# Row sums of squares from token-major rows, and a planner that only asks for order between matmuls of one PSUM tile

## The chip, the cores and the metric

The kernel runs on one core of a Trainium2 chip. The metric is the device time of one execution in microseconds (us), the median of several runs. The core's engines are TensorE (PE, with PEld for its weight loads), VectorE (DVE), ScalarE (ACT), GpSimd (POOL) and SyncE (SP); each runs its own instructions in program order and waits for the others by semaphores. ACT, POOL and SP also issue DMA transfers.

## The reference

One decoder layer on x of 2048 tokens by 1024 features, all in float32, cut to what matters here:

```
n    = rms_norm(x, norm_w)                 # x * rsqrt(mean(x*x) + 1e-6) * norm_w, per token
proj = n @ w_in                            # pool u, z; q, k, v, z of 4 heads; b, a (4 + 4 columns)
y_pool = pool_mixer(u, z)                  # causal means over 2, 4, 8, 16 tokens, a 128x128 map, SiLU gate
y_dn   = gated delta rule(q, k, v, b, a)   # 4 heads of 128, short convolution, a state per head
h    = x + concat(y_pool, y_dn) @ w_out
out  = rms_norm(h, final_norm_w)
```

The factor rsqrt(mean(x*x) + 1e-6) is one number per token. The projection doesn't wait for it: it multiplies x times norm_w by the weights, and the factor is applied to the result.

## The kernel before, in words

The 2048 tokens are two batches b of 1024, and a batch is two halves hf of 512. x comes feature-major (the input xT, features on partitions): `load_x` brings a half of a batch in four transfers of 512 KB (the first one in two pieces), `split_x` makes for each of its eight blocks of 128 features a rounded part nh (ACT, L518) and a remainder nl (DVE, L519). `project` adds into one PSUM tile ps, for each of these eight k, three matmuls of 128x512: nh by wh (L725), nl by wh (L726) and nh by wl (L727), where wh and wl are the two parts of a 128-column tile of the weight (wh from a transfer on POOL's queue, wl from ACT L716 and a transfer that adds).

The row sums: `square_x` squares each of the eight blocks on ACT (L527, L531) and adds it to the sum sacc on DVE (odd k) or POOL (even k, L533). `row_scale` sums sacc over the partitions with four one-column matmuls into pss (L538), takes the mean (DVE L542) and rsqrt (POOL L500), and makes a diagonal matrix dg per 128 tokens (DVE L549, it needs the identity, which is the first part of the constants cst). `broadcast` turns dg by a matmul into psr (L553) and ACT copies it to rb (L555): the factor of every token on all partitions. Everything that leaves a projection's PSUM tile is multiplied by rb, so the first of these waits for it. `gate_rows` makes the b and a columns in psba (L561, L562) with the weights whl, which ACT and DVE make from wba (L488, L489); `gate_scale` multiplies them by rb (ba, L566) and `gate_turn` transposes them on PE (L573).

After the projections of a head come its chunks of the delta rule, whose state passes through PE, ACT and DVE in turn (PE ch and ob, ACT nv, o and the squares sqj, DVE v and state; L993 to L1022). At the end the output projection works on pairs of token tiles in products M1 to M7, whose sums lie in the PSUM tiles psA to psD; DVE adds x (L1295), ACT squares with a sum (L1297), POOL takes the rsqrt (L500), and the scaled rows go out on SP's queue.

The order of the instructions is made by a planner in Python. The kernel gives pieces of work to `at(slot, fn, ...)`; they are traced by slot. The class `Planner` then plays the program by a table of costs (`costs`): each engine takes, of what is ready, the instruction with the earliest due time; PE takes whole runs (the matmuls of one piece), looking at most REACH = 24 runs ahead. An instruction counts as ready when all it depends on has ended by the table (`preds`) or, for some pairs, has begun (`begun`). The order that comes out is what each engine runs. It sets no time: on the chip an engine waits for what it really needs. Transfers on SP and ACT share eight lanes, each with a semaphore: a new transfer on a lane is issued when the last one on it has landed.

Of the kernel before, what the change touches and what calls it, by code (L numbers as in the profile page):

```python
# [7 lines left out]
F32 = mybir.dt.float32  # L8
# [29 lines left out]
L_RB = (5.5, 4.25, 5.25, 4.25)  # L38
L_MIX, WARM = 90, 11
L_ROW, L_GROW, L_SUMS, L_DEC = 3.0, 2.5, 2, 4.0  # L40
L_KK, L_Q, L_QK, L_SPLIT, L_W = 1.5, 6.5, 1.5, 20, 30
L_ROW0, L_SQ1, L_SQB, L_X, L_GR0, L_GR, L_GCOL = (16.0, 18.0), 13.5, -40, 44, 21.5, 5.5, 2.75
PAIRED = 2

X_TAGS = (
    (("dec", 4), ("dec", 4), ("dec", 4), ("kdec", 2)),
    (("dec", 4), ("kdec", 2), ("kT", 2), ("kT", 2)),
)
WO_TAGS = (("At",), ("Ai",), ("Tt", 2), ("vT",))
# [37 lines left out]
class Planner:  # L87
# [34 lines left out]
    def costs(self, i, outs, ins):  # L122
# [27 lines left out]
        if eng == "Pool":  # L150
            t = 600 if op == "TensorTensor" and n <= NC else {"TensorScalarAffineSelect": 620}.get(op, 0.95 * n if op == "Memset" else 2.5 * n + 20)
            return t, t + 30
# [11 lines left out]
    def run(self):  # L164
# [56 lines left out]
        after = [[] for _ in range(N)]  # L221
        for k, p in enumerate(preds):
            begun[k] -= p | {k}
            for j in p:
                succs[j].append(k)
            for j in begun[k]:
                after[j].append(k)
# [169 lines left out]
def hymba_kernel(  # L397
# [31 lines left out]
    def st(shape, dt, tag, bufs=1):  # L429
        return plan.tile(sp, shape, dt, tag, tag, bufs)  # L430
# [36 lines left out]
    def load_constants():  # L467
        plan.opening = len(plan.traced)
        tri = st([P, 2, P], F32, "X")
        for dst, src in (  # L470
            (cst, consts[:, 0:C_TMP]),
            (wba, w_ba),
# [49 lines left out]

    def square_x(k, env):
        xk = env["x"][k // 2][:, k % 2]
        if k == 0:
            env["ss"] = ss = st([P, HALF], F32, "sacc", 2)
            nc.scalar.activation(ss, xk, AF.Square)  # L527
        else:
            ss = env["ss"]
            sq = st([P, HALF], F32, "acc", 3)  # L530
            nc.scalar.activation(sq, xk, AF.Square)  # L531
            eng = nc.vector if k % 2 else nc.gpsimd
            eng.tensor_tensor(out=ss, in0=ss, in1=sq, op=ALU.add)  # L533

    def row_scale(env):
        ps = plan.tile(pd, [P, HALF], F32, "pd", "pss", 2, True)
        for j in range(NCH):
            nc.tensor.matmul(  # L538
                ps[:, j : j + 1], env["ss"][:, j * P : (j + 1) * P], ones[:, 0:1], start=True, stop=True
            )  # L540
        v = st([P, NCH], F32, "ms", 2)
        nc.vector.tensor_scalar(  # L542
            out=v, in0=ps[:, 0:NCH], scalar1=1.0 / D, scalar2=EPS, op0=ALU.mult, op1=ALU.add
        )
        r = st([P, NCH], F32, "rstd", 2)
        rsqrt(r, v)
        env["dg"] = dg = st([P, NCH, P], F32, "sacc", 2)
        for j in range(NCH):
            nc.vector.tensor_scalar(out=dg[:, j], in0=ident, scalar1=r[:, j : j + 1], scalar2=None, op0=ALU.mult)  # L549

# [120 lines left out]
    def at(slot, fn, *args):  # L671
        events.append((slot, len(events), fn, args))
# [434 lines left out]
    tri = []  # L1107
    at(-90, begin)
    at(-89, warm_up)
    at(-45, lambda: tri.append(load_constants()))  # L1110
    at(-1, lambda: prepare_constants(tri[0]))
    for b in range(NB):
# [21 lines left out]
        for hf in range(NHALF):  # L1134
# [4 lines left out]
            for k in range(KT):  # L1139
                at(base + 0.1 + k * (8 * PAIRED - 2) / KT, split_x, k, env)  # L1140
                at(base + (L_SQB if b else 4 + L_SQ1 * hf) + k * (8 * PAIRED - 2) / KT, square_x, k, env)
            base += 8 * PAIRED - 2
            base += L_ROW if b else L_ROW0[hf]
            at(base, row_scale, env)
            at(base + L_RB[b * NHALF + hf], broadcast, env)
# [403 lines left out]
```

## Time and profile before

| | us |
|---|---|
| median of 3 runs (lowest, highest) | 940.88 (939.42, 942.4) |
| the profiled execution | 942.56 |
| span of its profile | 940.9 |
| PE busy | 917.2 (97%) |
| DVE, ACT, POOL busy | 617.1 (66%), 471.1 (50%), 188.2 (20%) |

The span is the time between the first and the last record of the profile; 1.66 us of the execution lie around it. Starts are counted from the span's start. A row of a timeline gives the start, the time that the instruction took, its engine, its line, what it writes and reads, and in brackets how long its engine had been idle before it and what ended that. Matmuls overlap: two of 128x512 that follow one another start 0.23 us apart though each shows 0.39.

### The profile page before, as it was taken

Reading aid. Unit: us, or ns where it says so; the run is one execution under the profiler, and the core shown is the slowest. Engines: PE = TensorE matmul, PEld = TensorE weight load, DVE = VectorE, ACT = ScalarE, POOL = GpSimd, SP = SyncE. Lnnn points to the kernel's source line nnn. Section 1 sums busy time; section 2 is a strip of 40 time slices with the busy share of each in tenths; the row PEclk is TensorE's granted clock in tenths of the full one; section 3 lists DMA queues with packets and bytes.
Section 4 is the critical chain, followed back from the end, with each engine's and each line's share of the span. In section 5 each row is a group of like instructions: output and inputs, shape, how many; then the busy total and the mean of one; then the engine's idle time right before and its main releaser. Section 6 shows DMA issues by size and latency. Waiting matters only on the chain.

```text
span 940.9 us, 14732 instructions
## 1 busy us (share of the span) xinstructions
PE 917.2 (97%) x5226; PEld 739.0 (79%) x5226; DVE 617.1 (66%) x1637; ACT 471.1 (50%) x1225; POOL 188.2 (20%) x224
## 2 busy tenths in 40 slices
PE   8999999999999999999999999999999999999995
PEld 5678888778878878768887787887887788788884
DVE  7476867666758545855785675855854477976553
ACT  8348555464454345624945546545533345444442
POOL 3417210110110113312720121111011101112221
PEclk9999999999999999999999999999999999999998
DMA  8425564344333454433445244353248487376554
GB/s 291 106 57 115 132 167 104 65 96 92 85 91 95 122 181 138 109 74 83 102 95 125 56 88 107 71 107 95 60 111 259 121 230 227 128 187 161 153 112 123
DMA packets 82265, 115.81 MB, mean 123 GB/s; under 512 B 31888, under 2 KB 49552, under 8 KB 82192
## 3 DMA queue, kind: packets, MB, share of 16 engines
q0 software_dynamic: 17280, 56.89, 28.3%
q1 hardware_dynamic: 64480, 57.46, 19.8%
q8 instruction: 41, 0.67, 0.3%
q10 hardware_dynamic: 432, 0.53, 0.2%
q14 instruction: 32, 0.26, 0.1%
HBM read 92.83 MB, written 22.02 MB: 122 GB/s over the span
## 4 chain that ended last, share of the span: by engine, by line
PE 67%; issue 11%; DVE 8%; DMA 6%; POOL 3%; ACT 3%; SPq 1%; DVEq 0%; POOLq 0%; ACTq 0%
PE ps L725 13%; PE ps L727 12%; PE ps L726 12%; DMA wh<-in_w_in_dram 2%; PE psA L1403 2%; PE psA L1404 2%; PE psA L1402 2%; PE ch L1009 1%; PE ch L1015 1%; PE tp L817 1%; PE ch L993 1%; PE ob L1003 1%; PE kk L843 1%; PE psC L1404 1%; PE psC L1402 1%
## 5 line engine op out<-in xcount | busy, mean ns | idle before, releaser
L725 PE MATMUL ps<-nh,wh 128*128 128x512 f32 x768 | 325.9, 424 | 1.4 <-ACT wh L713 0.8
L726 PE MATMUL ps<-nl,wh 128*128 128x512 f32 x768 | 301.6, 393 | 2.2 <-DVE nl L519 2.1
L727 PE MATMUL ps<-nh,wl 128*128 128x512 f32 x768 | 301.6, 393 | 0.0
L727 PEld LDWEIGHTS ps<-nh,wl 128*128 128x128 f32 x768 | 144.6, 188 | 32.1 <-DVE wl L503 0.4
L725 PEld LDWEIGHTS ps<-nh,wh 128*128 128x128 f32 x768 | 145.4, 189 | 27.4 <-issue 1.7
L726 PEld LDWEIGHTS ps<-nl,wh 128*128 128x128 f32 x768 | 145.5, 189 | 27.1 <-DVE nl L519 4.5
L739 DVE SCALAR_TENSOR_TENSOR acc<-u,cw,acc 128x512 f32<-128x512 f32 x144 | 109.6, 761 | 17.2 <-ACT acc L737 15.3
L708 POOL DMA_DIRECT2D wh<-in_w_in_dram x40 | 23.2, 579 | 289.9 <-PE ps L727 278.3
L734 DVE TENSOR_TENSOR u<-ps,rb 128x512 f32<-128x512 f32 x48 | 33.1, 689 | 59.7 <-PE ps L727 59.6
L717 POOL DMA_DIRECT2D wl<-in_w_in_dram x40 | 35.1, 878 | 155.8 <-ACT wl L716 100.6
L716 ACT ACTIVATE wl<-wh 128x1024 fp32r<-128x1024 f32 x40 | 42.4, 1059 | 34.7 <-DMA wh<-in_w_in_dram 31.3
L896 DVE TENSOR_TENSOR tmp<-Ai,X 128x60 f32<-128x60 f32 (+24 forms) x248 | 53.5, 216 | 7.7 <-DMA Ai<-blocks 1.5
L902 DVE TENSOR_TENSOR X<-X,tmp 128x60 f32<-128x60 f32 (+24 forms) x248 | 53.7, 216 | 6.7
L737 ACT ACTIVATE acc<-u,cw 128x512 f32<-128x512 f32 x48 | 34.8, 724 | 42.3 <-DVE u L734 41.7
L1022 ACT ACTIVATE sqj<-v 128x128 f32<-128x128 f32 x64 | 19.8, 309 | 64.5 <-DVE v L1020 59.7
L1016 DVE SCALAR_TENSOR_TENSOR state<-state,ex,ch 128x128 f32<-128x128 f32 x64 | 22.0, 344 | 28.1 <-PE ch L1015 27.7
L1410 POOL DMA_DIRECT2D dec<-in_x_dram x23 | 20.0, 871 | 100.6 <-ACT dec L1409 58.9
L1011 ACT ACTIVATE nv<-ch,sm 128x128 f32<-128x128 f32 x64 | 23.6, 368 | 30.4 <-PE ch L1009 30.0
L824 ACT ACTIVATE sqj<-tp 128x128 f32<-128x128 f32 x128 | 33.6, 280 | 4.2 <-PE tp L817 3.9
L1005 ACT ACTIVATE o<-ob,ex 128x128 f32<-128x128 f32 x64 | 23.5, 367 | 13.7 <-PE ob L1003 13.2
L993 PEld LDWEIGHTS ch<-state,kT 128*128 128x128 f32 x128 | 22.5, 188 | 8.3 <-DVE state L1016 4.3
L1015 PEld LDWEIGHTS ch<-nv,kdec 128*128 128x128 f32 x128 | 19.7, 188 | 11.7 <-ACT nv L1011 11.0
(288 smaller groups left out, 1760.3 us busy)
## 6 DMA issues: line engine op xcount, KB each, us to landing
wh<-in_w_in_dram POOLq DMA_DIRECT2D x40, 512.0 KB, 3.9
wl<-in_w_in_dram POOLq DMA_DIRECT2D x40, 512.0 KB, 5.6
y_dram<-yt SPq DMA_DIRECT2D x32, 256.0 KB, 3.1
out_dram<-dec SPq DMA_DIRECT2D x14, 512.0 KB, 4.5
dec<-in_x_dram POOLq DMA_DIRECT2D x23, 256.0 KB, 4.2
Ai<-blocks SPq DMA_DIRECT2D x32, 128.0 KB, 2.7
yr<-y_dram SPq DMA_DIRECT2D x8, 512.0 KB, 4.5
dec<-in_xT_dram SPq DMA_DIRECT2D x7, 512.0 KB, 6.9
```

The source lines that it names most:

```text
L716: nc.scalar.activation(w["lo"], w["hi"].bitcast(F32), AF.Copy, scale=-1.0)
L717: nc.gpsimd.dma_start(w["lo"], w_in[et], accum_op=ALU.add)
L725: nc.tensor.matmul(ps, w["hi"][:, k], nh[:, k], start=(k == 0), stop=False)
L726: nc.tensor.matmul(ps, w["hi"][:, k], nl[:, k], start=False, stop=False)
L727: nc.tensor.matmul(ps, w["lo"][:, k], nh[:, k], start=False, stop=(k == KT - 1))
L734: nc.vector.tensor_tensor(out=ub[:, HALO:], in0=ps, in1=rb, op=ALU.mult)
L737: nc.scalar.activation(acc, ub[:, HALO:], AF.Copy, scale=cw[:, ci, CONV - 1 : CONV])
L739: nc.vector.scalar_tensor_tensor(out=acc, in0=ub[:, h0 + j : h0 + j + HALF], scalar=cw[:, ci, j : j + 1], in1=acc, op0=ALU.mult, op1=ALU.add,)
L824: nc.scalar.activation(junk, tp[:, j], AF.Square, accum_out=dst[:, c : c + 1])
L896: nc.vector.tensor_tensor(out=tmp[:, 0:n, 0:w], in0=Ai[:, j, j + 1 : BS].unsqueeze(1).to_broadcast([P, n, w]), in1=X[:, 0:n, j : j + 1].to ...
L902: nc.vector.tensor_tensor(out=X[:, 0:n, j + 1 : BS], in0=X[:, 0:n, j + 1 : BS], in1=tmp[:, 0:n, 0:w], op=ALU.subtract)
L993: nc.tensor.matmul(ch[:, 0], res["kT"][:, t], S, start=True, stop=True)
```

## The change

Three things are changed.

- Row sums. `square_x` and the matmuls into pss are gone. `load_rows` loads x once more, token-major (128 tokens on partitions, 1024 features, 512 KB per transfer, four per half, on SP's queue), and `square_rows` squares such a tile on ACT with a sum along the row, which gives the four columns of ms. In the first batch the tiles take buffers that are not yet used (ROW_TAGS); in the second all eight go through the one buffer yr1, one after the other. `row_scale` now only makes the mean and the rsqrt, in the second batch 36 slots earlier than before; `row_diagonal` makes dg where `row_scale` made it.
- The identity (in cst) is loaded at the start on ACT's queue, not among the constants on SP's.
- The planner. A matmul that adds to or follows another on PE by data now counts as ready when the other has begun, by the table, and no longer when it has ended. And a small TensorTensor on POOL (the rsqrt) costs 430 + 160 n ns in the table for n columns, 600 before.

```diff
+ROW_TAGS = (
+    (("Ai",), ("At",), ("v0",), ("vT",)),
+    (("Tt", 2), ("Tt", 2), ("yr1",), ("Ai",)),
+)
...
-            t = 600 if op == "TensorTensor" and n <= NC else {"TensorScalarAffineSelect": 620}.get(op, 0.95 * n if op == "Memset" else 2.5 * n + 20)
+            t = 430 + 160 * n if op == "TensorTensor" and n <= NC else {"TensorScalarAffineSelect": 620}.get(op, 0.95 * n if op == "Memset" else 2.5 * n + 20)
...
         for k, p in enumerate(preds):
+            if eng[k] == "PE":
+                own = {j for j in p if eng[j] == "PE"}
+                p -= own
+                begun[k] |= own
             begun[k] -= p | {k}
...
         for dst, src in (
-            (cst, consts[:, 0:C_TMP]),
             (wba, w_ba),
...
-    def square_x(k, env):
...
+    def load_rows(b, hf, j, env):
+        env["xt", j] = xt = st([P, D], F32, *(ROW_TAGS[hf][j] if b == 0 else ("yr1",)))
+        t0 = b * TB + hf * HALF + j * P
+        nc.sync.dma_start(xt, x[t0 : t0 + P, :])
+
+    def square_rows(j, env):
+        if j == 0:
+            env["ms"] = st([P, NCH], F32, "ms", 2)
+        xt = env["xt", j]
+        nc.scalar.activation(xt, xt, AF.Square, accum_out=env["ms"][:, j : j + 1])
 
     def row_scale(env):
-        ps = plan.tile(pd, [P, HALF], F32, "pd", "pss", 2, True)
-        for j in range(NCH):
-            nc.tensor.matmul(
-                ps[:, j : j + 1], env["ss"][:, j * P : (j + 1) * P], ones[:, 0:1], start=True, stop=True
-            )
...
+        v = env["ms"]
+        nc.vector.tensor_scalar(out=v, in0=v, scalar1=1.0 / D, scalar2=EPS, op0=ALU.mult, op1=ALU.add)
+        env["r"] = r = st([P, NCH], F32, "rstd", 2)
         rsqrt(r, v)
+
+    def row_diagonal(env):
         env["dg"] = dg = st([P, NCH, P], F32, "sacc", 2)
...
+    at(-79.5, lambda: nc.scalar.dma_start(cst, consts[:, 0:C_TMP]))
...
-                at(base + (L_SQB if b else 4 + L_SQ1 * hf) + k * (8 * PAIRED - 2) / KT, square_x, k, env)
...
-            at(base, row_scale, env)
+            for j in range(NCH):
+                at(base - L_XT + 4 * j if b else -67 + 5 * hf + 0.1 * j, load_rows, b, hf, j, env)
+                at(base - L_XT + 8 + 4 * j if b else 4 + 8 * hf + j, square_rows, j, env)
+            at(base - L_XT + 24 if b else base, row_scale, env)
+            at(base, row_diagonal, env)
```

What the planner makes of this is seen from the order of the instructions. SP's queue in the opening, after the loads of xT and of the first weight (dec, kdec and kT hold xT), before:

```order
L513 DMA kT<-in_xT_dram 128x2x512 x2
L481 DMA cst<-in_consts_dram 128x192
L481 DMA wba<-in_w_ba_dram 128x64
L481 DMA pw<-in_pool_w_dram 128x512
L481 DMA psc<-in_pool_scale_dram 128x4
L481 DMA dtb<-in_dt_bias_dram 128x4
```

and after (Ai, At, v_146 and vT hold the rows of the first half, both Tt, yr_154 and the later Ai those of the second):

```order
L520 DMA kT<-in_xT_dram 128x2x512 x2
L533 DMA Ai<-in_x_dram 128x1024
L533 DMA At<-in_x_dram 128x1024
L533 DMA v_146<-in_x_dram 128x1024
L533 DMA vT<-in_x_dram 128x1024
L533 DMA Tt<-in_x_dram 128x1024 x2
L533 DMA yr_154<-in_x_dram 128x1024
L488 DMA wba<-in_w_ba_dram 128x64
L533 DMA Ai<-in_x_dram 128x1024
L488 DMA pw<-in_pool_w_dram 128x512
```

Seven loads of rows now stand ahead of wba. ACT in the opening, from the second half's split of x on, before:

```order
L518 ACTIVATE nh<-dec,nw 128x512
L518 ACTIVATE nh<-kdec,nw 128x512 x2
L518 ACTIVATE nh<-kT,nw 128x512 x2
L488 CAST whl<-wba 128x8x8
L518 ACTIVATE nh<-kT,nw 128x512 x2
L716 ACTIVATE wl<-wh 128x1024
L531 ACTIVATE acc<-dec 128x512
L527 ACTIVATE sacc<-dec 128x512
```

and after:

```order
L719 ACTIVATE wl<-wh 128x1024
L525 ACTIVATE nh<-kT,nw 128x512 x2
L539 ACTIVATE Ai,ms<-Ai 128x1024
L539 ACTIVATE At,ms<-At 128x1024
L495 CAST whl<-wba 128x8x8
L539 ACTIVATE v_146,ms<-v_146 128x1024
L539 ACTIVATE vT,ms<-vT 128x1024
L525 ACTIVATE nh<-kT,nw 128x512 x2
L539 ACTIVATE Tt,ms<-Tt 128x1024 x2
```

The cast of wba stands ahead of the last two squares of the first half and of the last two splits (k = 6, 7 of the second half). PE at the program's end, the last nine matmuls before:

```order
L1402 MATMUL psA<-At,wh 128x512
L1403 MATMUL psA<-Tt,wh 128x512
L1404 MATMUL psA<-At,wl 128x512
L1402 MATMUL psC<-nh,rb 128x512
L1403 MATMUL psC<-nl,rb 128x512
L1404 MATMUL psC<-nh,acc 128x512
L1402 MATMUL psA<-Ai,wh 128x512
L1403 MATMUL psA<-vT,wh 128x512
L1404 MATMUL psA<-Ai,wl 128x512
```

and after (psC's three rows then stand three times more, up to the end):

```order
L1409 MATMUL psA<-Ai,wh 128x512
L1410 MATMUL psA<-vT,wh 128x512
L1411 MATMUL psA<-Ai,wl 128x512
L1409 MATMUL psC<-nh,rb 128x512
L1410 MATMUL psC<-nl,rb 128x512
L1411 MATMUL psC<-nh,acc 128x512
```

Before, the two tiles took turns to the end; after, psA is finished twelve matmuls ahead of it. The same holds in the projections: among all neighbours in PE's order that belong to a projection or to the output products there were 809 changes of the PSUM tile, and are 196.

## Rows read from the trace of the kernel before

**Rows 1.** The page: busy time, share of the span and instructions of each engine.
```profile
PE 917.2 (97%) x5226; PEld 739.0 (79%) x5226; DVE 617.1 (66%) x1637; ACT 471.1 (50%) x1225; POOL 188.2 (20%) x224
```
**Rows 2.** Timeline, PE in the opening: start, duration, instruction, idle before and releaser.
```profile
5.97 0.50 PE L725 MATMUL ps<-nh,wh 128*128 128x512 f32 x1 [0.75 <-ACT wh L713]
...
14.60 0.50 PE L726 MATMUL ps<-nl,wh 128*128 128x512 f32 x1 [0.72 <-DVE nl L519]
...
18.94 0.50 PE L726 MATMUL ps<-nl,wh 128*128 128x512 f32 x1 [0.64 <-DVE nl L519]
...
21.67 0.40 PE L727 MATMUL ps<-nh,wl 128*128 128x512 f32 x1
...
21.90 0.95 PE L538 MATMUL pss<-ones,sacc 128*128 128x1 f32 x8
...
23.02 0.39 PE L726 MATMUL ps<-nl,wh 128*128 128x512 f32 x1
...
51.68 0.39 PE L725 MATMUL ps<-nh,wh 128*128 128x512 f32 x1
```
**Rows 3.** Timeline, the other engines in the opening.
```profile
10.53 0.34 SPq L481 DMA_DIRECT2D wba<-in_w_ba_dram  x1
...
12.10 2.44 DVE L519 SCALAR_TENSOR_TENSOR nl<-kdec,nw,nh 128x512 fp32r<-128x512 f32 x2
...
12.39 1.60 POOL L533 TENSOR_TENSOR sacc<-sacc,acc 128x512 f32<-128x512 f32 x1 [9.09 <-ACT acc L531]
...
21.10 1.41 DVE L519 SCALAR_TENSOR_TENSOR nl<-kdec,nw,nh 128x512 fp32r<-128x512 f32 x2
...
21.13 0.23 ACT L488 CAST whl<-wba 128x64 fp32r<-128x64 f32 x1
...
23.99 1.62 POOL L500 TENSOR_TENSOR rstd<-ms,mhalf 128x4 f32<-128x4 f32 x1 [3.96 <-DVE ms L542]
...
25.64 0.89 DVE L549 TENSOR_SCALAR sacc<-cst,rstd 128x128 f32<-128x128 f32 x4 [0.27 <-POOL rstd L500]
```
**Rows 4.** DMA, 0 to 40 us: GB/s by microsecond; issues, KB each, us to landing.
```profile
GB/s 0 23 199 332 404 352 397 410 401 361 397 397 393 393 387 375 352 371 348 163 365 33 0 0 0 0 0 66 143 221 214 23 5 0 8 0 12 197 329 244
...
wba<-in_w_ba_dram SPq DMA_DIRECT2D x1, 32.0 KB, 7.3
```
**Rows 5.** Groups by line and form: count, busy us, mean ns, idle before, releasers.
```profile
L716 ACT ACTIVATE wl<-wh 128x1024 fp32r<-128x1024 f32 x40 | 42.4, 1059 | 34.7 <-DMA wh<-in_w_in_dram 31.3 <-issue 3.3
...
L1297 ACT ACTIVATE t<-dec 128x512 f32<-128x512 f32 x32 | 20.2, 632 | 17.2 <-DVE dec L1295 16.9
...
L1297 ACT ACTIVATION_READ_ACCUMULATOR t<-dec 128x1 f32 x32 | 6.0, 187 | 0.0
...
L500 POOL TENSOR_TENSOR rki<-vk,mhalf 128x8 f32<-128x8 f32 x8 | 13.8, 1720 | 14.5 <-DVE vk L834 14.4
```
**Rows 6.** Timeline, PE at the start of the second batch.
```profile
406.18 0.39 PE L727 MATMUL ps<-nh,wl 128*128 128x512 f32 x1
408.10 0.42 PE L573 MATMUL tp<-cst,ba 16*128 16x16 f32 x4 [1.54 <-DVE ba L566]
408.45 1.05 PE L538 MATMUL pss<-ones,sacc 128*128 128x1 f32 x8
```
**Rows 7.** Windows there: length, busy (count) by engine, granted clock, DMA share, GB/s.
```profile
410.50:413.00 2.50, 2.50 (x7) 1.97 (x6) 0.88 (x4) 0.00 (x0) 0.89 (x1) 0.50 0.27 54
```
**Rows 8.** Timeline, ACT inside a head's chain of chunks.
```profile
357.26 1.66 ACT L531 ACTIVATE acc<-dec 128x512 f32<-128x512 f32 x3
```
**Rows 9.** Timeline, the end of the program.
```profile
930.36 0.40 PE L1404 MATMUL psA<-Ai,wl 128*128 128x512 f32 x1
930.79 1.29 DVE L1295 TENSOR_TENSOR dec<-psA,dec 128x512 f32<-128x512 f32 x2
...
934.33 1.02 POOL L500 TENSOR_TENSOR ro<-vo,mhalf 128x1 f32<-128x1 f32 x1 [0.17 <-DVE vo L1310]
```
**Rows 10.** Timeline, PE at a chunk of the second batch that waits for DVE.
```profile
655.99 0.49 PE L1009 MATMUL ch<-rho,Tt 128*128 128x128 f32 x2 [0.70 <-DVE rho L995]
```

More of the change, by code (lines that the diff above doesn't have):

```diff
@@ L38 @@
 L_RB = (5.5, 4.25, 5.25, 4.25)
-L_MIX, WARM = 90, 11
+L_MIX, L_XT, WARM = 90, 60, 11
 L_ROW, L_GROW, L_SUMS, L_DEC = 3.0, 2.5, 2, 4.0
 L_KK, L_Q, L_QK, L_SPLIT, L_W = 1.5, 6.5, 1.5, 20, 30
-L_ROW0, L_SQ1, L_SQB, L_X, L_GR0, L_GR, L_GCOL = (16.0, 18.0), 13.5, -40, 44, 21.5, 5.5, 2.75
+L_ROW0, L_X, L_GR0, L_GR, L_GCOL = (16.0, 18.0), 44, 21.5, 5.5, 2.75
 PAIRED = 2
@@ L521, in split_x @@
         )
-    def square_x(k, env):
[L524 to L533, printed above, removed]
-    def row_scale(env):
-        ps = plan.tile(pd, [P, HALF], F32, "pd", "pss", 2, True)
-        for j in range(NCH):
-            nc.tensor.matmul(
-                ps[:, j : j + 1], env["ss"][:, j * P : (j + 1) * P], ones[:, 0:1], start=True, stop=True
-            )
[L541 to L545, printed above, removed]
+    def load_rows(b, hf, j, env):
[7 more added lines that the diff above has]
+        nc.scalar.activation(xt, xt, AF.Square, accum_out=env["ms"][:, j : j + 1])
+    def row_scale(env):
+        v = env["ms"]
+        nc.vector.tensor_scalar(out=v, in0=v, scalar1=1.0 / D, scalar2=EPS, op0=ALU.mult, op1=ALU.add)
+        env["r"] = r = st([P, NCH], F32, "rstd", 2)
         rsqrt(r, v)
+    def row_diagonal(env):
         env["dg"] = dg = st([P, NCH, P], F32, "sacc", 2)
         for j in range(NCH):
-            nc.vector.tensor_scalar(out=dg[:, j], in0=ident, scalar1=r[:, j : j + 1], scalar2=None, op0=ALU.mult)
+            nc.vector.tensor_scalar(
+                out=dg[:, j], in0=ident, scalar1=env["r"][:, j : j + 1], scalar2=None, op0=ALU.mult
+            )
     def broadcast(env):
```

## The prediction

> **What bounds the kernel now.** I read the page first. PE is busy for 917.2 of 940.9 us [rows 1], so 23.7 us are all that PE's waits can give back; beyond that, time falls only with work taken off PE, with a half clock avoided, or with the ends of the program. DVE, ACT and POOL have room on average, so what they lose or gain counts only where PE waits for them. I then read PE's timeline for the places where it does. In the opening it waits several times for a split of x, nl, 0.72 us at 14.60 and 0.64 us at 18.94 [rows 2]; the two nl on DVE at 12.10 take 2.44 us with a POOL addition running through them, where the two at 21.10 take 1.41 without one [rows 3]. At the start of the second batch PE stands still for 1.54 us until ba comes, does two pieces of small matmuls, and then the granted clock is 0.50 (the lower level, 1.2 GHz) for the 2.5 us from 410.5 [rows 6, 7]. The end has 10.5 us after the start of the last matmul at 930.36 [rows 9]. The rest of the idle time lies in small waits between chunks, such as 0.70 us at 655.99 [rows 10].
>
> The sum is made against the profiled execution's span of 940.9 us; its 942.56 us are 1.7 above the median of 940.88, and I carry the difference over to the median.
>
> **Work taken off PE: pss.** The block of 21.90 lies between two ordinary matmuls, 21.67 and 23.02, which are 1.35 us apart with one other between them; two ordinary steps are 0.46, so the block costs 0.9 us [rows 2]. There are four such blocks: −1.8 us in the opening, −1.8 at the second batch. The ACT squares, DVE additions and POOL additions that go are off the path but for the slow nl pairs, which are the waits of 0.72 and 0.64: −1.4 in the opening, if nothing later ends there.
>
> **The opening: something later does end there.** The order of SP's queue puts seven row loads of 512 KB ahead of wba. SP's transfers land in the order of the queue: wba was issued at 10.53 and landed 7.3 us later, 17.8, though it is 32 KB [rows 3, 4]; what it waited for is the bulk ahead of it. Bytes ahead of it were 5.24 MB of xT and first weights, 0.1 of cst: at 385 GB/s, about the mean of the full slices, 13.9 us, plus 2.6 us that the first slices lack, gives 16.5, and with part of a weight on POOL's queue 17.2, 0.6 short of the landing [rows 4]. After the change 10.05 MB are ahead (5.24 + 0.1 + seven rows 3.67 + one weight and its remainder 1.04): 26.1 + 2.6 + 0.6 = 29.3 us. Without the remainder ahead it is 27.9; at 350 GB/s, the slices in which POOL's queue moves too, 31.9. I take 29.3, from the slices that are most.
>
> The Trainium skill, page "DMA: Bandwidth & Descriptors", section "Anatomy of one DMA — SWDGE (gpsimd) path", gives the moving part of a transfer as its bytes over 436 GB/s. That is an estimate of 1.2 us for 512 KB, where the slices here, at 352 to 410 GB/s, give 1.36; by the page wba would land 3.0 us earlier and the sum below would be 934.0.
>
> Before, the cast of wba on ACT at 21.13 waited for nothing [rows 3]. Now ACT stands at it from about 22 until 29.3, and behind it in ACT's order are the last two squares of the first half and the splits k = 6, 7 of the second half. A square of 128x1024 with a sum is not in the trace. The nearest rows are 1.06 us for a 128x1024 activation without a sum, and 0.63 + 0.19 for 128x512 with one [rows 5]: between 1.06 and 1.64, I take 1.2, the first plus the reading of the sum less their overlap. So: cast ends 29.7, two squares 32.1, mean on DVE 32.4, POOL's rsqrt 1.62, dg 0.89 [rows 3] and hand-offs of 0.1 each: dg at 35.1. PE has 78 projection matmuls before it needs the split k = 6. Before, pss at 21.90 followed 48 of them, 10.9 us at 0.228 from 5.97, so 5.0 us of waits lay there, and 1.4 of them goes: 5.97 + 17.8 + 3.6 = 27.4 [rows 2]. It gets that split at about 32.9, idle for 5.5 us, then runs 6 matmuls and waits for dg. In before, 120 projection matmuls, two psr, 32 psba, four transposes and one pm are done when the row at 51.68 starts. After psr (0.9 us) at 36.0, 68 of these matmuls (15.5 us at 0.228) and 2.2 us of the rest are left: 53.7. An idle stretch of 5.5 us is longer than the one at 408, after which 2.5 us ran at the half clock, 1.25 of it lost [rows 6, 7]: +1.3, so 55.0. The opening costs 55.0 − 51.68 = **+3.3 us**, its 1.8 and 1.4 already given away. Bounds: 27.9 and no half clock, +0.6; 31.9, +5.9.
>
> cst on ACT's queue is 0.1 MB, 0.25 us earlier on a full queue, and counted above.
>
> **The second batch.** rstd is made 36 slots earlier and dg no longer waits behind squares and additions, so ba should come about as PE gets there. That ends 1.6 us of the stretch 406.18 to 408.10 [rows 6]; without idle time and the one-column matmuls the clock should not fall, 1.3 us [rows 7]; pss 1.8. Together **−4.7**. The rows' transfers (eight of 512 KB, one after the other through one buffer) and squares (8 × 1.2 = 9.6 us of ACT) stand in place of 16 squares of about 0.55 [rows 8], on ACT inside the last head's chunks; I cost them at nothing: PE has projections of the next heads to run beside that chain, and the squares of before stood in it too. If that cover is gone it is the second rival.
>
> **The end.** psA is finished twelve matmuls early, so its two additions on DVE (1.29 us for two, [rows 9]) are done before PE ends, and one addition, square and rsqrt are left. In before the last rsqrt starts at 934.33 [rows 9]. Now: last matmul at its start + 0.4, addition 0.65, square and sum 0.8 [rows 5], two small DVE steps 0.3, hand-offs 0.25: 2.4 after the last matmul's start against 4.0: **−1.5**, between −0.8 (POOL's or DVE's turn comes late) and −2.
>
> **The planner, everywhere else.** Small rsqrts are priced 1710 ns for 8 columns, where the rows show 1720 [rows 5], not 600; so the plan can give PE other work in that time, and waits such as the one at 655.99, behind DVE work that itself waits for the rsqrt, can go [rows 10]. Against it, the whole order is new, and projections now run to their end one after another, which hands DVE its tiles in another rhythm. No row prices that. A gain is bounded by the idle time outside the three places, 23.7 less 10.1 at the end, 1.5 at the second batch and 5.0 in the opening, some 7 us, most of it single waits that a new order can as well make as mend. I take **−1**, between −3 and +3.
>
> **Sum.** 940.9 + 3.3 − 4.7 − 1.5 − 1.0 = 937.0 us of span, 3.9 less; on the median **937.0 us**. The likeliest case's own range is 932 to 942.
>
> **Rivals.**
> 1. *wba doesn't hold PE.* It lands in time, or ACT's next work isn't needed. Then the opening keeps its 1.8 and 1.4: −3.2 in place of +3.3, **930.5**. For it: in before the small loads cost nothing. Against: wba stands behind 3.67 MB more on a queue that is full from 3 us on [rows 4].
> 2. *Slower: the squares of the second batch sit in the state's chain.* They are twice as long as those of before (1.2 against 0.55), and ACT runs them between the o, nv and sqj steps of the last head's chunks, where each next chunk waits for the last. Eight times 1.2 on the path is +9.6: **946.6**. It decides (slower by over 0.3%) from 0.84 us per square. For it: the transfers go one by one through one buffer, and a square whose row is late holds ACT longer than 1.2. Against: at 357.26 three squares of before, 1.66 us together [rows 8], stood there and PE had other matmuls.
> 3. *The boundary's wait stays.* ba is late for another reason than dg (the psba matmuls or the splits that they need); 1.6 of idle and 1.3 of half clock are not won: **939.9**, within 0.3%. For it: DVE makes ba in its own order, behind all the splits of the second half [rows 6]. Against: rb, which ba needs too, came from dg. That the change doesn't do what it says is part of this: rsqrt early, nothing gained.
>
> **How the numbers follow.** A measurement of this kernel can tell about 0.3% from no change, 2.8 us: faster is under 938.1, slower over 943.7. Forecast 0.53 (0.31 of it faster, 0.22 same), rival 1 0.14 (faster), rival 2 0.12 (slower), rival 3 0.21 (0.04 faster, 0.17 same). Faster 0.49, same 0.39, slower 0.12. The range 930 to 943 leaves out some half of rival 1 and all of rival 2, 0.19.
>
> **What would show it.** In the profile after: the cast of wba idle on ACT until about 29 us and PE idle before the nl or nh of k = 6 for 5 to 6 us, and the matmul that stood at 51.68 near 55 (right), or no such wait (rival 1). A granted clock of 0.5 after that gap. At the second batch, tp of ba without idle time before it and the clock at 1.0; a wait of 1.5 us there speaks for rival 3. At the end, the last rsqrt 2.4 us after the last matmul's start. In the last head of the first batch, PE waiting for nv behind a square speaks for rival 2. I would be wrong above all if small waits of several us in sum came or went all over the middle, since that term rests on one row and a new order.

## The result, and the profile after

The changed kernel takes 935.6 us (median of six runs, 933.28 to 936.74), the kernel before 941.5 in the same comparison: a ratio of 0.993, with a 95% interval of 0.9914 to 0.9945. That is 5.9 us less, where 3.9 less (937.0) was forecast. The profiled execution took 933.28 us, with a span of 931.6, so it is the fastest of the six, and the two profiles lie 9.3 us apart, not 5.9. What is read from them below adds up to 9.3; what holds for the medians is said where the two differ. In the experiments one execution of the planner alone, 946.4 us, was a slow one and is left out of its median and ratio.

The page of the changed kernel, busy time by engine (it answers to [rows 1]):

```profile
PE 909.4 (98%) x5194; PEld 738.5 (79%) x5194; DVE 606.9 (65%) x1621; ACT 475.1 (51%) x1227; POOL 171.6 (18%) x212
```

PE has 32 records less (the pss matmuls) and is busy 7.8 us less. Its idle time is 22.2 us after 23.7: the change hardly took idle time away in sum, it moved it. Where to, the timelines show. First ACT in the opening (start, duration, instruction, idle before it and what ended that), against [rows 3]:

```profile
30.83 0.24 ACT L495 CAST whl<-wba 128x64 fp32r<-128x64 f32 x1 [7.86 <-DMA wba<-in_w_ba_dram]
30.98 1.05 ACT L539 ACTIVATE v<-v 128x1024 f32<-128x1024 f32 x1
31.94 0.19 ACT L539 ACTIVATION_READ_ACCUMULATOR v<-v 128x1 f32 x1
32.03 1.04 ACT L539 ACTIVATE vT<-vT 128x1024 f32<-128x1024 f32 x1
...
33.07 1.32 ACT L525 ACTIVATE nh<-kT,nw 128x512 fp32r<-128x512 f32 x2
```

ACT stands idle for 7.86 us at the cast until wba lands, and two squares and the splits k = 6, 7 follow it. The loads of v and vT had landed before wba, since they stand ahead of it on SP's queue: the squares run back to back, 1.05 us apart. PE in the same stretch, against [rows 2]; the last row is the matmul that stood at 51.68 in the kernel before (called the anchor below), with the same work done ahead of it but for pss:

```profile
10.47 0.79 PE L728 MATMUL ps<-nh,wh 128*128 128x512 f32 x1 [2.41 <-ACT nh L525]
...
33.83 0.79 PE L728 MATMUL ps<-nh,wh 128*128 128x512 f32 x1 [4.99 <-ACT nh L525]
34.61 0.80 PE L729 MATMUL ps<-nl,wh 128*128 128x512 f32 x1
35.20 0.63 PE L730 MATMUL ps<-nh,wl 128*128 128x512 f32 x1
35.63 0.63 PE L728 MATMUL ps<-nh,wh 128*128 128x512 f32 x1
...
36.91 1.42 PE L556 MATMUL psr<-sacc,ones 128*128 128x512 f32 x2
...
56.02 0.39 PE L728 MATMUL ps<-nh,wh 128*128 128x512 f32 x1
```

And the window behind the long wait (length, busy time and count by engine, granted clock, DMA share, GB/s):

```profile
33.80:38.00 4.20, 4.17 (x9) 2.65 (x9) 2.25 (x6) 3.70 (x7) 2.59 (x3) 0.53 0.00 0
```

PE waits 4.99 us for the split, then runs 4.2 us at a granted clock of 0.53, close to the lower level: the step from 35.20 to 35.63 is 0.43 us. The anchor starts 4.3 us later than before. There is a second wait, 2.41 us at 10.47, that the prediction doesn't have, with a granted clock of 0.54 from 12 to 14 us behind it. The first weight on POOL's queue (512 KB) now goes out at once, at 1.42, since no additions stand ahead of it on POOL:

```profile
1.42 0.72 POOL L711 DMA_DIRECT2D wh<-in_w_in_dram  x1
```

Before it was issued at 13.94, behind the POOL addition of [rows 3]. Its bytes now move beside those of the first tiles of xT; that this is the wait's cause is asked of a run below.

At the second batch, against [rows 6, 7], PE goes through without idle time:

```profile
408.54 0.39 PE L730 MATMUL ps<-nh,wl 128*128 128x512 f32 x1
408.86 0.42 PE L576 MATMUL tp<-cst,ba 16*128 16x16 f32 x4
```

And the window behind it, of 10 us (columns as above; the clock is the third from the right):

```profile
410.00:420.00 10.00, 10.00 (x43) 7.09 (x42) 1.44 (x2) 2.50 (x3) 0.00 (x0) 1.00 0.01 2
```

The transposes of ba start at 408.86, 0.76 us after those of before with exactly the same matmuls done; 4.3 us behind at 56 have become 0.8. The clock stays at 1.00 where it fell to 0.50. At the end, against [rows 9]:

```profile
922.67 0.40 PE L1411 MATMUL psC<-nh,acc 128*128 128x512 f32 x1
...
925.14 0.93 POOL L507 TENSOR_TENSOR ro<-vo,mhalf 128x1 f32<-128x1 f32 x1 [1.47 <-DVE vo L1317]
```

The last rsqrt starts 2.5 us after the last matmul's start, 4.0 before, and the span ends 8.9 us after it, not 10.5.

So the 9.3 us between the profiles are: opening +4.3, both pss blocks of the second batch −1.8, its wait and half clock −3.3, the end −1.6, and −6.9 that lie in the middle, 1.1 of it before the second batch and 5.8 behind its start. The medians are only 5.9 us apart. The experiment with mean and rsqrt in their old slot has, as it turned out, the order of the changed kernel on every engine, so it gives a second profile, of an execution of 935.76 us, close to the median. There the anchor stands at 57.88, the transposes of ba at 411.32 and the last matmul at 925.07: opening +6.2, the second batch and the end as above, middle −6.4 (5.9 of it behind the start of the second batch). What differs from one execution to the other is for the most part the opening.

### The profile page after: what moved, and what is told of

Its sections match the earlier page's. It is cut to its first block, busy times and chain, and to the rows that moved or that the text cites. A ratio compares the mean times of both kernels' runs of the same rounds, so it can differ in the third digit from the quotient of the medians.

```text
span 931.6 us, 14634 instructions
## 1 busy us (share of the span) xinstructions
PE 909.4 (98%) x5194; PEld 738.5 (79%) x5194; DVE 606.9 (65%) x1621; ACT 475.1 (51%) x1227; POOL 171.6 (18%) x212
## 4 chain that ended last, share of the span: by engine, by line
PE 83%; DMA 5%; DVE 5%; ACT 3%; issue 2%; SPq 1%; POOL 0%; POOLq 0%; DVEq 0%; ACTq 0%
PE ps L728 16%; PE ps L730 16%; PE ps L729 16%; PE psA L1410 2%; PE ch L1018 2%; PE psA L1411 2%; PE psA L1409 2%; PE tp L820 2%; PE ch L1012 2%; PE ch L996 2%; PE pso L1297 2%; PE pso L1295 2%; PE pso L1296 2%; PE ob L1022 1%; PE ob L1006 1%
## 5 line engine op out<-in xcount | busy, mean ns | idle before, releaser
L742 DVE SCALAR_TENSOR_TENSOR acc<-u,cw,acc 128x512 f32<-128x512 f32 x144 | 113.6, 789 | 19.0 <-ACT acc L740 16.8
L720 POOL DMA_DIRECT2D wl<-in_w_in_dram x40 | 35.1, 877 | 174.0 <-ACT wl L719 140.2
L737 DVE TENSOR_TENSOR u<-ps,rb 128x512 f32<-128x512 f32 x48 | 33.1, 689 | 43.9 <-PE ps L730 43.7
L1304 ACT ACTIVATE t<-dec 128x512 f32<-128x512 f32 x32 | 20.2, 632 | 17.3 <-DVE dec L1302 16.8
```

Source lines behind the costliest of these rows:

```text
L720: nc.gpsimd.dma_start(w["lo"], w_in[et], accum_op=ALU.add)
L737: nc.vector.tensor_tensor(out=ub[:, HALO:], in0=ps, in1=rb, op=ALU.mult)
L742: nc.vector.scalar_tensor_tensor(out=acc, in0=ub[:, h0 + j : h0 + j + HALF], scalar=cw[:, ci, j : j + 1], in1=acc, op0=ALU.mult, op1=ALU.add,)
```

## The experiments

All times are medians, and each is set against runs of the kernel before on the same chip; "ratio" is to that kernel. A table at the end of the section sets the profiles side by side at three places. The first four ask for the terms of the sum.

**wba early.** The cast's load goes out at the start on ACT's queue.

```diff
-            (wba, w_ba),
...
-    at(-79.5, lambda: nc.scalar.dma_start(cst, consts[:, 0:C_TMP]))
+    at(-79.5, lambda: (nc.scalar.dma_start(cst, consts[:, 0:C_TMP]), nc.scalar.dma_start(wba, w_ba)))
```

> The changed kernel, with wba loaded at the start on ACT's queue right behind cst instead of behind the row loads on SP's. Theory (the wait for wba on ACT is what the opening pays): the cast no longer waits 7.9 us, PE's stretch of 4.99 us idle at 33.8 and the half clock after it go, 6 to 7.5 us less than the changed kernel's 935.6, so 928 to 930. Rival (the squares v and vT and their loads hold the splits as long): most of the idle time stays, within 2 us of 935.6.

Measured: 930.8 us, ratio 0.9893 (0.9879 to 0.9908), 4.8 less than the changed kernel. ACT and PE then:

```profile
12.68 0.23 ACT L494 CAST whl<-wba 128x64 fp32r<-128x64 f32 x1
...
33.87 0.21 ACT L499 ACTIVATE nega<-nega 128x4 f32<-128x4 f32 x1 [2.98 <-DMA nega<-in_a_log_dram]
33.99 0.57 ACT L557 COPY rb<-psr 128x512 f32<-128x512 f32 x1
...
35.33 0.40 PE L563 MATMUL psba<-nh,whl 128*16 128x512 f32 x1 [1.03 <-DVE u L765]
```

The cast waits for nothing and PE's 4.99 us and its half clock are gone, so the load's place behind the rows was the cause: shown. The anchor comes at 50.51, 5.5 us before that of the changed kernel. The gain falls short of 6 to 7.5 in two places. In the opening the same thing happens once more: nega, 2 KB, also stands behind the rows on SP's queue; ACT waits 2.98 us for it, with psr done, and rb behind it. And a wait of PE for a late kT, which the changed kernel has too, is followed here by a stretch at the lower clock (the second row is a window, columns as above):

```profile
115.92 0.66 PE L819 MATMUL tp<-cst,kT 128*128 128x128 f32 x4 [2.07 <-ACT kT L749]
...
117.00:120.00 3.00, 3.00 (x9) 2.34 (x8) 1.31 (x6) 2.33 (x11) 0.55 (x1) 0.51 0.68 203
```

In the changed kernel the wait is 2.03 us, at 121.46, and the clock behind it stays at 1.00:

```profile
121.40:126.00 4.60, 4.54 (x26) 3.99 (x27) 2.65 (x8) 3.57 (x16) 0.55 (x1) 1.00 0.69 187
```

**The planner alone**, and **the rows alone**: the two halves of the change, each put on the kernel before.

```diff
+            if eng[k] == "PE":
+                own = {j for j in p if eng[j] == "PE"}
+                p -= own
+                begun[k] |= own
...
-            t = 600 if op == ...
+            t = 430 + 160 * n if op == ...
```

> The kernel before with the two planner edits alone (order between matmuls of PE by begin, price of POOL's small rsqrt). Theory of the forecast: the end gives 1.5 and the middle 1, pss, the opening and the boundary stay: 2.5 less than before, 939.0. Rival (the planner carries the gain of 7 us that the changed kernel shows in the middle): 6 to 9 less, 932 to 935.

> The changed kernel with the two planner edits undone: row sums from token-major loads and the early identity alone. Here the cast of wba stands behind the splits of x on ACT, so the opening should gain 3.2 (pss 1.8, slow splits 1.4) and the second batch 4.7, the end nothing: 7.9 less than before, 933.6. Rival (the middle's gain comes with the rows, since DVE and POOL have less work there): 927 to 930. Rival (rows hold something else in the opening): 937 or more.

Measured: the planner alone 938.1, ratio 0.9964 (0.9944 to 0.9983), 3 to 3.5 less than before, within a microsecond of what was expected, though its executions spread from 932.3 to 940.7. The rows alone **947.5**, ratio 1.0067 (1.0045 to 1.0089): 6.4 slower, where 7.9 faster was expected; only the rival that something else is held in the opening, 937 or more, has the sign. The two don't add up: −3 and +6 give −6 together. The profile is of an execution of 944.06 us, 3.4 below the median, so it shows only a part of the loss. In it the rows alone lose in two places. The first is the opening: the anchor stands at 53.34, 1.7 later than before, where 3.2 earlier was expected. PE's waits there, and the window between them:

```profile
11.65 0.80 PE L724 MATMUL ps<-nh,wh 128*128 128x512 f32 x1 [3.50 <-ACT nh L521]
...
33.07 1.13 PE L552 MATMUL psr<-sacc,ones 128*128 128x512 f32 x2 [1.57 <-DVE sacc L546]
```

```profile
11.60:18.00 6.40, 6.35 (x14) 4.69 (x15) 6.40 (x11) 6.04 (x10) 0.00 (x0) 0.50 1.06 389
```

The first weight goes out at 1.42 here too, PE waits 3.5 us and then runs 6.4 us at the lower clock, and later waits for dg. The second place is ahead of the second batch:

```profile
347.32 0.50 PE L726 MATMUL ps<-nh,wl 128*128 128x512 f32 x1 [2.31 <-DMA wl<-in_w_in_dram]
...
379.04 0.50 PE L726 MATMUL ps<-nh,wl 128*128 128x512 f32 x1 [4.16 <-DMA wl<-in_w_in_dram]
```

The transfer that the first of them waits for, among the DMA issues (queue, operation, KB, us from issue to landing):

```profile
wl<-in_w_in_dram POOLq DMA_DIRECT2D x1, 512.0 KB, 10.9
```

PE waits twice for a weight's remainder, 6.5 us, and the granted clock is at its lower level for some 3 us after the second. The transfer took 10.9 us, where the median of the kernel before is 5.6: it was issued at 336 us among 1.5 MB of xT, a tile of rows and a second weight. In the changed kernel the same piece of work has no such wait.

**Mean and rsqrt of the second batch in their old slot.**

```diff
-            at(base - L_XT + 24 if b else base, row_scale, env)
+            at(base, row_scale, env)
```

> The changed kernel with the second batch's mean and rsqrt back in the slot of the diagonal. Theory (ba came late because rstd and dg did): the idle time before the transposes of ba (1.5) and the half clock (1.3) come back, 938 to 939. Rival (the rsqrt's place in the order is no matter once no squares on POOL and DVE stand ahead of it): as the changed kernel, 935.6.

Measured: 935.6, ratio 0.9944 (0.9929 to 0.9959), the same as the changed kernel. The trace shows why it had to be: the planner gives every engine the same order as in the changed kernel, and still places the two rsqrts early, at 345.55 and 376.56, where the changed kernel has them at 343.56 and 374.53.

```profile
376.56 1.06 POOL L507 TENSOR_TENSOR rstd<-ms,mhalf 128x4 f32<-128x4 f32 x1
...
411.32 0.42 PE L576 MATMUL tp<-cst,ba 16*128 16x16 f32 x4
```

The 36 slots move nothing. That leaves the rows' squares, made early and without additions, as what brings rstd forward; no run asks that by itself. This profile also says something on the changed kernel's spread: with the same order, the wait for wba was longer here.

```profile
32.01 0.24 ACT L495 CAST whl<-wba 128x64 fp32r<-128x64 f32 x1 [8.86 <-DMA wba<-in_w_ba_dram]
...
35.01 0.79 PE L728 MATMUL ps<-nh,wh 128*128 128x512 f32 x1 [7.02 <-ACT nh L525]
```

PE lost 7.0 us where the changed kernel's profile has 5.0, and the anchor is 1.9 later; behind the start of the second batch the two profiles agree to 0.1 us. So of the 2.4 us between these two spans 1.9 lie in the opening.

The next four ask for the planner's two edits and for what the rows did.

**The price undone**, and **order by end again**, each in the changed kernel.

```diff
-            t = 430 + 160 * n if op == ...
+            t = 600 if op == ...
```

> The changed kernel with the price of POOL's small rsqrt back at 600 ns. Theory of the forecast (the right price is worth about 1 us of small waits in the middle): 936.6, 1 more than the changed kernel. Rival (the price moves only neighbours, no wait): 935.6, with the same small waits behind the rsqrt of a head. The opening keeps its wait for wba in both.

```diff
-            if eng[k] == "PE":
-                own = {j for j in p if eng[j] == "PE"}
-                p -= own
-                begun[k] |= own
```

> The changed kernel with order between matmuls of PE again by end, not by begin; the price stays. The run with the rows alone was 947.5, with waits for a weight's remainder wl of 2.5 and 4.3 us near 347 and 379, where its transfer took 10.9 us beside the rows and xT of the second batch. Theory (it is the order by begin that keeps that stretch free): about 946 to 947.5, the same waits, and the output tiles alternate again. Rival (the price does it): 936 to 938, no such waits.

Measured: without the price 939.5 (ratio 0.9968, 0.9953 to 0.9983), without order by begin 939.3 (0.9976, 0.9959 to 0.9994). Either edit undone costs some 4 us, and neither expectation holds in size: each is worth four times what the price was given, and order by begin alone doesn't explain the 947.5. Without the price the opening is that of the changed kernel (anchor at 57.49, between its two profiles) and the loss lies behind it. The largest part that the trace shows is in three rows:

```profile
357.14 1.06 ACT L539 ACTIVATE yr<-yr 128x1024 f32<-128x1024 f32 x1 [2.11 <-DMA yr<-in_x_dram]
...
358.19 0.35 ACT L1014 ACTIVATE nv<-ch,sm 128x128 f32<-128x128 f32 x1
...
358.59 0.49 PE L1018 MATMUL ch<-nv,kdec 128*128 128x128 f32 x2 [1.81 <-ACT nv L1014]
```

A square of the second batch waits 2.11 us for its row, nv of a chunk stands behind it on ACT, and PE waits 1.81 us for nv. That is the mechanism of the second rival, in one place and not in eight; in the changed kernel's order no square does it.

With order by end again the opening is no later (anchor at 54.55). The profile is of an execution of 942.21 us, 2.9 above the median; in it the loss is in three places. Ahead of the second batch PE waits 2.12 us for a Tt from ACT (1.05 at the same place in the kernel before, with the clock at 1.00 behind it), and then the clock is at its lower level for 10 us, which costs 5; the wait for wl of the rows alone comes back as well, at 1.19 us:

```profile
338.54 1.06 PE L959 MATMUL p<-cst,Tt 64*64 64x64 f32 x8 [2.12 <-ACT Tt L952]
...
379.82 0.49 PE L726 MATMUL ps<-nh,wl 128*128 128x512 f32 x1 [1.19 <-DMA wl<-in_w_in_dram]
```

```profile
338.50:348.50 10.00, 9.96 (x47) 7.29 (x48) 1.79 (x6) 3.73 (x8) 1.93 (x2) 0.50 0.96 273
```

The stretch from the transposes of ba to the last matmul is 3.4 us longer than in the changed kernel. And the span ends 10.5 us after the last matmul's start, as before the change, not 8.9. So order by begin, and not the rows, makes the end's gain: shown.

What order by begin brings by itself is seen in the output products, 155 us in which the work is the same matmul throughout. The window of the kernel before (columns as above):

```profile
760.00:915.00 155.00, 154.64 (x675) 126.28 (x674) 114.76 (x168) 73.88 (x140) 23.81 (x28) 1.00 0.63 171
```

The changed kernel:

```profile
760.00:915.00 155.00, 155.00 (x683) 127.94 (x682) 111.62 (x166) 71.59 (x141) 28.57 (x31) 1.00 0.63 169
```

The changed kernel with order by end again:

```profile
760.00:915.00 155.00, 154.64 (x677) 126.67 (x676) 115.36 (x169) 74.13 (x140) 24.61 (x28) 1.00 0.62 171
```

With tiles run one after the other PE starts 681 (the planner alone) to 683 matmuls in 155 us, with tiles that alternate 675 to 677: six to eight steps of 0.23, 1.4 to 1.8 us. Some 0.8 us of it are two stops, which all kernels ordered by end have and none ordered by begin. In the kernel before:

```profile
804.82 0.39 PE L1290 MATMUL pso<-nh,wl 128*128 128x512 f32 x1
805.56 0.50 PE L1288 MATMUL pso<-nh,wh 128*128 128x512 f32 x1 [0.36 <-DVE dec L1295]
...
815.46 0.39 PE L1403 MATMUL psC<-qT,wh 128*128 128x512 f32 x1
815.78 0.50 PE L1404 MATMUL psC<-kT,wl 128*128 128x512 f32 x1
816.12 0.39 PE L1402 MATMUL psA<-nh,wh 128*128 128x512 f32 x1
```

Four steps in these places take 0.74, 0.34, 0.32 and 0.34 us. The rest is ordinary steps that are about a nanosecond longer, within a tile as much as from one tile to the other (228.7 and 229.1 ns on average before, 227.5 and 226.9 after). So that alternating by itself makes a step longer isn't shown, and why they differ the rows don't say.

**The rows alone, without the second batch's transfers.** POOL fills the buffer instead.

```diff
+        if b == 0:
             nc.sync.dma_start(xt, x[t0 : t0 + P, :])
+        else:
+            nc.gpsimd.memset(xt, 1.0)
```

> The run with the rows alone, with the eight row transfers of the second batch left out: POOL fills the buffer with ones instead, ACT's squares stay, so the second batch's row sums are not those of x. Theory (the rows' transfers crowd those of the weights): the waits for wl near 347 and 379, 6.8 us together, go, so about 940 to 941. Rival (the squares on ACT hold the cast of wl): the waits stay, 946 to 947.5.

Measured: 945.9, ratio 1.0038 (1.0025 to 1.0051). The wait near 347 is gone, the one near 380 is not:

```profile
380.58 0.50 PE L729 MATMUL ps<-nh,wl 128*128 128x512 f32 x1 [4.63 <-DMA wl<-in_w_in_dram]
```

Its DMA issues, a tile of xT and the weight's remainder issued behind it:

```profile
dec<-in_xT_dram SPq DMA_DIRECT2D x1, 512.0 KB, 7.8
wl<-in_w_in_dram POOLq DMA_DIRECT2D x1, 512.0 KB, 10.0
```

So neither theory: without the rows' transfers the first wait is gone, but here wl takes 10.0 us without any row on the queue, issued 0.3 us behind the second of two tiles of xT; in the kernel before it was issued half a microsecond ahead of them and took 6.5. That points to which of two transfers is issued first, at a place where the weight is needed as soon as it lands; no run changes that alone.

**wba early, and the first weight late.** Eight fills of its own buffer, unpriced, stand ahead of its load on POOL.

```diff
+            if not held:
+                held.append(et)
+                for i in range(8):
+                    nc.gpsimd.memset(w["hi"].bitcast(F32), 0.0)
             nc.gpsimd.dma_start(w["hi"], w_in[et])
```

> The run with wba early (930.8), and the first weight on POOL's queue issued some 8 us later, behind eight fills of its own buffer; all other instructions in their order. In the changed kernel that weight goes out at 1.4 us, before at 13.9, and the third piece of xT lands at 9.7 instead of 7.8. Theory (its 512 KB delay the first x and weight, and PE's two early waits of 1.5 and 1.3 us): 1 to 2 less, 929 to 930. Rival (the bytes are due in the opening anyway and the wait comes back before the rows or that weight): 930.8.

Measured: 931.8, ratio 0.9875 (0.985 to 0.9899): no gain on 930.8, as the rival has it (the ratio is 0.2% lower, with intervals that overlap). The early waits are gone: PE waits 0.64 us at 6.83 where wba early has 1.44 there and 0.92 at 10.64, and the clock is 1.00 up to 34 us. So the first weight's bytes were their cause, and most likely that of the 2.41 us at 10.47 in the changed kernel: with constants first, below, the same step cuts a wait of 2.47 us near 10 to 1.15. But PE then waits for the same nega (idle 2.91 on ACT), 3.61 us before psba at 35.44, and gets a half clock after it.

The last four ask what the opening's floor is, and what the second batch's transfers cost.

**Constants first**, and **constants first with the first weight late**.

```diff
-        plan.opening = len(plan.traced)
...
-    at(-45, lambda: tri.append(load_constants()))
+    at(-68, lambda: tri.append(load_constants()))
+    at(-45, lambda: setattr(plan, "opening", len(plan.traced)))
```

> The changed kernel with all small constants (wba, nega, dtb, cw, psc, pw, the triangles) ahead of the row loads on SP's queue. Theory (any small load behind the rows holds ACT: with wba early it is nega, 3.0 us, and rb stands behind it): no wait for wba or nega on ACT, PE's 1.2 us for psba goes too, 928 to 930. Rival (0.5 MB more ahead of the rows makes the row sums that much later, so dg and rb come no earlier): 930.8 or more.

> The same, and the first weight on POOL's queue issued some 8 us later as in the run with wba early. There PE was 3.9 us ahead of the kernel before at its third ten of work, and lost it in a wait of 3.6 us behind nega and a half clock after it. Theory (that wait was all that took the gain): 3 to 6 us less than with wba early, 925 to 928. Rival (the rows themselves are next: squares, rsqrt, dg): 929 to 931.

Measured: 929.7 (ratio 0.9864, 0.9832 to 0.9896), within what was expected but not apart from the rival's 930.8 by its interval, and 931.5 (0.9886, 0.9848 to 0.9925), the rival's value. No small load holds ACT any more; the rows do, and PE waits for dg in both. The anchors, 53.42 and 52.97, are no earlier than with wba early. ACT and PE with constants first:

```profile
27.27 1.06 ACT L538 ACTIVATE At<-At 128x1024 f32<-128x1024 f32 x1 [2.18 <-DMA At<-in_x_dram]
...
30.26 1.06 ACT L538 ACTIVATE v<-v 128x1024 f32<-128x1024 f32 x1 [1.84 <-DMA v<-in_x_dram]
...
35.69 1.66 PE L555 MATMUL psr<-sacc,ones 128*128 128x512 f32 x2 [2.04 <-DVE sacc L549]
```

PE with the weight late as well:

```profile
35.21 1.48 PE L555 MATMUL psr<-sacc,ones 128*128 128x512 f32 x2 [4.40 <-DVE sacc L549]
```

**The first batch's rows not loaded**, in the kernel of 931.5, and **the second batch's rows not loaded**, in the kernel of 930.8. DVE or POOL fills the buffer, as above.

```diff
-        nc.sync.dma_start(xt, x[t0 : t0 + P, :])
+        if b == 1:
+            nc.sync.dma_start(xt, x[t0 : t0 + P, :])
+        else:
+            nc.vector.memset(xt, 1.0)
```

> The run with the constants first and the late weight (931.5, PE 4.4 us idle before psr of the first half), with the eight row transfers of the first batch left out: DVE fills the buffers with ones, the squares stay, so the first batch's row sums are not those of x. Theory (what is left in the opening is the rows' own 4 MB on the queue ahead of dg): PE's wait before psr goes and the half clock after it, 5 to 7 less, 925 to 927. Rival (something else comes as late: the weights, or the splits of x): 929 or more.

```diff
-        nc.sync.dma_start(xt, x[t0 : t0 + P, :])
+        if b == 0:
+            nc.sync.dma_start(xt, x[t0 : t0 + P, :])
+        else:
+            nc.gpsimd.memset(xt, 1.0)
```

> The run with wba early (930.8), with the eight row transfers of the second batch left out: POOL fills the buffer with ones, the squares stay, so the second batch's row sums are not those of x. Theory of the forecast (in the changed order these transfers and squares are hidden): 930.8, within 1.5. Rival (they delay weights or chunks there as in the run with the rows alone): 2 to 5 less.

Measured: 925.6 (ratio 0.983, 0.9815 to 0.9845) and 931.0 (0.9887, 0.9869 to 0.9904); both theories hold. Without the first batch's rows there is no wait of PE over 0.3 us in the opening behind 10 us, and the clock is 1.00:

```profile
28.00:34.00 6.00, 6.00 (x27) 3.80 (x26) 4.53 (x13) 3.49 (x7) 2.29 (x3) 1.00 0.55 168
```

So reading the first batch twice costs 5 to 6 us in a kernel in which no small load holds ACT (5.9 by the medians, 5.3 by the ratios, 5.7 by the anchors), and the second batch's eight transfers cost nothing in the changed order; their squares stayed, so what those cost isn't asked.

Of the kernels that load all rows, wba early, 930.8, and all constants first, 929.7, are the fastest. Their intervals overlap.

**The profiles side by side.** At each of the three places PE has done the same matmuls in all of them but for pss, so what lies between two places can be compared. Starts in us; the first is the anchor, the second the transposes of ba in the second batch.

| kernel | anchor | tp of ba | last matmul | from tp to last |
|---|---|---|---|---|
| before | 51.68 | 408.10 | 930.36 | 522.3 |
| changed | 56.02 | 408.86 | 922.67 | 513.8 |
| changed, second profile (rsqrt in old slot) | 57.88 | 411.32 | 925.07 | 513.8 |
| wba early | 50.51 | 405.61 | 919.39 | 513.8 |
| wba early, first weight late | 53.35 | 408.91 | 922.70 | 513.8 |
| constants first | 53.42 | 406.81 | 920.51 | 513.7 |
| constants first, first weight late | 52.97 | 406.67 | 920.40 | 513.7 |
| the same, no rows in the first batch | 47.31 | 401.19 | 915.07 | 513.9 |
| wba early, no rows in the second batch | 50.38 | 406.80 | 920.60 | 513.8 |
| price undone | 57.49 | 413.65 | 928.90 | 515.3 |
| order by end again | 54.55 | 412.76 | 930.01 | 517.3 |
| planner alone | 50.62 | 409.89 | 926.07 | 516.2 |
| rows alone | 53.34 | 413.43 | 931.84 | 518.4 |

The last column hardly changes among kernels that have the rows and both planner edits, whatever their opening. It is 8.5 us shorter than before: one pss block 0.9, the half clock 1.7, and the middle's 5.8. Of these 5.8 undoing the price brings back 1.4 and undoing order by begin 3.4. So behind the start of the second batch the middle's gain is for the most part the planner's: shown.

## Why the prediction was right

It forecast 937.0 with a range of 930 to 943; 935.6 was measured. The second batch and the end came out as forecast, and so did the opening's path but for one step. That the sum is so close is in part luck: the opening lost more than was forecast and the middle gained more, and these two errors offset each other. Of its terms:

- **Opening, +3.3; measured +4.3 and +6.2 in the two profiles**, the second above its bound of +5.9. The path is right: the cast idle until 30.8 (29.3 by the sum over bytes; 32.0 in the second profile), the split at 33.1 to 33.8 (32.9), PE idle 5.0 (5.5), psr at 36.9 (35.1), a half clock behind the wait. One step isn't: PE doesn't wait for dg. Squares (1.05 from start to start, 1.2 taken) and rsqrt (1.04, 1.62 taken) are shorter than forecast and dg ends at 35.4; the six matmuls ahead of psr take 3.1 us at the lower clock and hold it. So the half clock was underpriced: 4.2 us at 0.53 lose 2 us, not 1.3. Missing was the 2.41 us wait at 10.47, which cost nothing by itself, since PE only waited less later. The run with wba early shows the cause; rival 1 falls.
- **Second batch, −4.7; measured −5.1** (two pss blocks 1.8, wait 1.6, half clock 1.7, of which the window of [rows 7] shows 1.3). The size is right, one reason isn't: the 36 slots do nothing. The cost of the eight transfers, put at nothing, is confirmed by leaving them out (931.0 for 930.8); that of the squares isn't tested by itself.
- **End, −1.5; measured −1.6**, 2.5 us from last matmul to last rsqrt (2.4 forecast). The planner alone shows it too: its last matmul starts at 926.07, the last rsqrt at 928.54; with order by end again it is gone.
- **Middle, −1, between −3 and +3; measured −6.9 and −6.4 in the two profiles.** This is the term that was mis-sized. Its working priced one chunk's wait, named the rest of the planner's effect as open and bounded a gain by PE's idle time. The runs show in its place 5.8 us behind the start of the second batch, most of it the planner's by the two runs that undo its edits: 1.8 us in the output products, and single waits that come and go with the order (PE is idle for 2.6 us between 415 and 760 before, 0.4 after). More than half of the 5.8 is not idle time at all but matmuls that follow one another sooner, which the bound leaves out. The wait of [rows 10] is not among PE's longer waits after the change, and with the price undone a wait of 0.70 us for rho comes back, so the price does what was said; but undoing it costs 3.9 us and not 1, since the whole order moves. The new order has its own: 2.03 us at 121.46 for a kT that ACT finishes late:

```profile
121.46 0.66 PE L820 MATMUL tp<-cst,kT 128*128 128x128 f32 x4 [2.03 <-ACT kT L750]
```

- **Rival 2** exists, as the trace without the price shows (1.81 us behind a late row), but in no place of the changed order. **Rival 3** falls: tp waits for nothing.
- That the rows alone would be *slower* was in no rival. The prediction summed two edits as if each kept its value beside the other; with the rows alone the opening comes 4.9 us later than was summed, and two waits for a weight and a half clock take 8 more. That these two waits are absent from the changed order is shown; without order by begin a shorter one, 1.19 us, comes back, without the price none, so which edit keeps them away is only in part shown.

Where the remaining single waits of the middle come from in each order, and 1 us of the 5.8, was not followed further.

## What to carry to other kernels

A load's place in a queue is part of its cost: a load of 32 KB that one instruction waits for was worth 4.8 us ahead of the bulk loads, since what it holds is whatever stands behind that instruction on its engine. Moving all small loads ahead, 0.5 MB, didn't shorten the opening further. Freeing an engine that stood between two transfers (here POOL's additions ahead of a weight) moves the transfer, so ask where its bytes go. And with an order made by a planner, an edit's value is that of the whole new order: measure halves of a change before crediting either, expect single waits of 1 to 4 us to come and go, and compare profiles at places where the same work is done, which tells a stretch that changed from one that only starts later.

## What the runs showed of the hardware that was not expected

- A square of 128x1024 with a sum along the row costs no more than one without: 1.05 us from start to start (30.98 to 32.03), with the reading of the sum (0.19) inside it; 1.06 is the duration of a plain activation of that size [rows 5].
- After 5.0 us without work PE ran 4.2 us at a granted clock of 0.53; the wait of 1.5 us in the kernel before was followed by 2.5 us at 0.50 [rows 6, 7]. The length of a wait doesn't tell what the clock does after it: behind 2.12 us came 10 us at 0.50 (order by end again), behind 2.07 us 3 us at 0.51 (wba early), and behind 2.03 us at the same piece of work none (the changed kernel, 1.00).
- POOL's rsqrt of four columns took 1.62 us in the opening before [rows 3], 1.04 in the opening and 1.04 and 1.06 at the second batch after the change.
